# A 64-byte pad ahead of the weight pool in a one-core hybrid decoder block

## Chip, cores and metric

The kernel runs on one core of a Trainium2 chip. The metric is device time in microseconds (us) of one execution. Before the change it is 2321.66 us, the median of three runs (2320.70 to 2322.68).

## What is computed

A decoder block over 256 tokens of width 2048: a SwiGLU feed-forward half step, a gated merge of differential attention and a gated linear recurrence, a second feed-forward half step, and a gated embedding. Cut to its matrix products:

```python
x = x + 0.5 * swiglu(rmsnorm(x, g1), w_gate, w_up, w_down)     # 2048 -> 2 x 5632 -> 2048
proj = rmsnorm(x, g2) @ w_in                                   # 2048 -> 11264
y_a = diff_attention(q, k, v) @ w_branch_a                     # 1024 -> 2048
y_b = hgrn2(hq, hf, hi, hg) @ w_branch_b                       # 1024 -> 2048
x = x + (sigmoid(gate_a) * y_a + sigmoid(gate_b) * y_b) @ w_out
x = x + 0.5 * swiglu(rmsnorm(x, g3), w_gate2, w_up2, w_down2)
x = x + sigmoid(rmsnorm(x, g4) @ w_ple_gate) * rmsnorm(p @ w_ple_proj, g5)
```

Everything is float32. The weights are about 420 MB, and each is read once.

## The kernel before

**The weight stream.** All weights are read in one order of use, the list `plan`, in groups of 256 input rows by 512 output columns (512 KB). `prep` (L103) handles one group: SyncE starts a DMA into `raw`, ScalarE rounds it into `wh` (L114), and VectorE writes the rounding remainder into `wl` (L115). It runs three groups ahead of their use (`AHEAD`). The pool `wp`, which holds five buffers of `raw` and four each of `wh` and `wl`, is the second pool that the program opens; the first, `base`, holds what lives through the whole program.

**The product.** An activation is split in the same way into a rounded part and a remainder, both transposed so that features stand on partitions: `AH`/`AL` for the normed stream, `hH`/`hL` for the hidden layer of a feed-forward, `yaH`/`yaL` and `ybH`/`ybL` for the branch inputs, `mH`/`mL` for the merged branches, `pH`/`pL` for the embedding input. `group` (L141 to L150) then issues, for each k-tile of 128 features and each of the two tiles of 128 tokens, three matmuls into the same 128x512 accumulator: `wh` under the activation's rounded part (L148), `wl` under the same (L149), `wh` under its remainder (L150). So a group is 12 matmuls. The activation slice of 128x128 is the stationary operand, which a weight load (LDWEIGHTS) puts into the array ahead of each matmul; the weights, 512 columns of float32r or 2048 bytes on each partition, are the moving operand. `product` strings the groups of one 512-column chunk together; `last_product` does the very last chunk partly in 256-column halves.

**Side work.** Everything else (scaling of accumulators, transposes, attention, recurrence) is cut into generator tasks. One piece of each runs between two groups of the stream (`advance`), so TensorE has the next group's matmuls queued behind it. The order is written out by the program, engine by engine; no scheduler changes it.

**Where tiles lie.** A pool gives each tag a place in SBUF in the order in which the tags first appear, in steps of 32 bytes per partition, and the pools follow each other. A tile keeps one byte offset on all 128 partitions. The lines that the change touches are L295 and L296, where the first `AH`/`AL` pair and `ss4` are made in `base`, and L335, where `gsub` is made in the pool `mid`.

Of the kernel before, what the change touches and what calls it, by code (L numbers as in the profile page):

```python
# [20 lines left out]
P = 128  # L21
# [27 lines left out]
def block_kernel(ctx: ExitStack, tc: tile.TileContext, a: dict, out: bass.AP):  # L49
# [3 lines left out]
    base = ctx.enter_context(tc.tile_pool(name="base", bufs=1))  # L53
# [8 lines left out]
    def T(pool, shape, tag, dt=F32, **kw):  # L62
        uid[0] += 1
        return pool.tile(shape, dt, tag=tag, name=f"{tag}_{uid[0]}", **kw)
# [4 lines left out]
    def ccol(c):  # L69
        return slice(c * NB, (c + 1) * NB)  # L70

# [1 line left out]
    plan = []  # L73

    def add(w, chunks, groups):
# [39 lines left out]
            nc.vector.tensor_tensor(wl[:, ks, :], raw[:, ks, :], wh[:, ks, :].bitcast(F32), op=ALU.subtract)  # L115
        ready[n] = (wh, wl)

# [1 line left out]
    tasks = []  # L119
    owed = [False]  # L120

# [55 lines left out]
                group(at[0] + i, act, 2 * groups - 1, [d])  # L177
            yield d

# [1 line left out]
    def split(H, L, src, gain=None):  # L181
        if gain is None:
            nc.scalar.copy(H, src)  # L183
            nc.vector.tensor_tensor(L, src, H.bitcast(F32), op=ALU.subtract)  # L184
        else:
            nc.scalar.activation(H, src, AF.Copy, scale=gain)  # L186
            nc.vector.scalar_tensor_tensor(L, src, gain, H.bitcast(F32), op0=ALU.mult, op1=ALU.subtract)
# [34 lines left out]
    def new_act():  # L222
        return T(base, [P, KD, SEQ], "AH", F32R), T(base, [P, KD, SEQ], "AL", F32R)

    def new_ss4():
        return T(base, [P, NT, 4], "ss4", bufs=2)
# [20 lines left out]
    def ffn(gu, down, act, gain_next):  # L247
        with tc.tile_pool(name=gu, bufs=1) as fp:
            hH = T(fp, [P, DFF // P, SEQ], "hH", F32R)
            hL = T(fp, [P, DFF // P, SEQ], "hL", F32R)  # L250

            def hidden(acc, c):
                if c == 0 and rs[0] is None:
                    early = T(fp, [P, NT, NB], "early")
                    for tt in range(NT):
                        nc.scalar.copy(early[:, tt, :], acc[tt])
                    acc = [early[:, tt, :] for tt in range(NT)]
                while rs[0] is None:
                    yield
                h = []  # L260
                for tt in range(NT):
                    s = T(fp, [P, HALF], "s", bufs=2)
                    nc.scalar.activation(s, acc[tt][:, :HALF], AF.Silu, scale=rs[0][:, tt : tt + 1])  # L263
                    h.append(T(fp, [P, HALF], "h", bufs=4))
                    nc.vector.scalar_tensor_tensor(  # L265
                        h[tt], acc[tt][:, HALF:], rs[0][:, tt : tt + 1], s, op0=ALU.mult, op1=ALU.mult
                    )
                yield
                two_k_tiles(lambda tt, kt: h[tt][:, (kt - 2 * c) * P : (kt - 2 * c + 1) * P], hH, hL, 2 * c)

            for c in range(DFF // HALF):
                acc = product(gu, c, KG, act)
                spawn(hidden(acc, c))
            nact = new_act()
            ss4 = new_ss4()
            for c in range(D // NB):
                acc = product(down, c, FG, (hH, hL))
                spawn(residual(acc, c, 0.5, ss4, nact, gain_next, set_rs if c == 3 else None))
        return nact

    # ------------------------------------------------------------------ first FFN
    gains = T(base, [P, 4, KD], "gains")
    nc.sync.dma_start(gains, a["gains"])
    neghalf = T(base, [P, 16], "neghalf")
# [8 lines left out]
    ident = T(base, [P, P], "ident")  # L293
    x = T(base, [P, NT, D], "x")
    act = new_act()  # L295
    ss4 = new_ss4()  # L296

    def load_xT(g):
# [26 lines left out]
    spawn(first_sums())  # L325
    act = ffn("gu1", "down1", act, gains[:, G_MIX])

    # ------------------------------------------------------------------ token mixing
    mid = ctx.enter_context(ExitStack())
    mp = mid.enter_context(tc.tile_pool(name="mid", bufs=1))  # L330
    GA = T(mp, [P, NT, D], "GA")
    V = T(mp, [P, NT, NH * VD], "V")
    yaH = T(mp, [P, NH, SEQ], "yaH", F32R)
    yaL = T(mp, [P, NH, SEQ], "yaL", F32R)
    gsub = T(mp, [P, 1], "gsub")  # L335
    nc.vector.tensor_scalar(gsub, small[:, S_SUB : S_SUB + 1], 1.0 - LAMBDA_INIT, None, op0=ALU.mult)

    def mix(m):
# [27 lines left out]
    with tc.tile_pool(name="att", bufs=1) as ap:  # L366
        qT = T(ap, [P, NH, SEQ], "qT")
        kT = T(ap, [P, NH, SEQ], "kT")
        dv = T(ap, [P, NT, NH * VD], "dv")
        bias = T(ap, [P, NH, SEQ], "bias")  # L370
# [55 lines left out]
                yield  # L426
            have.add(key)

        # the queries of a tile stand in reversed order from qT to aT, as the rows of the bias do
        PARTS = ((0, slice(0, SEQ), slice(0, SEQ)), (1, slice(SEQ, 3 * P), slice(P, SEQ)))  # L430

        def head(h, ya):
# [304 lines left out]
            spawn(residual(acc, c, 1.0, ss4, act, gains[:, G_FFN2], set_rs if c == 3 else None))  # L737
    mid.close()

    # ------------------------------------------------------------------ second FFN  # L740
    act = ffn("gu2", "down2", act, gains[:, G_PLE])

    # ------------------------------------------------------------------ per-layer embedding
    with tc.tile_pool(name="ple", bufs=1) as pp:
        pT = T(pp, [P, 2, SEQ], "pT")
        nc.gpsimd.dma_start(pT, a["pT"])
# [49 lines left out]
        drain()  # L796


# [1 line left out]
def _blocks(w):  # L800
    k, n = w.shape
    return np.ascontiguousarray(w.reshape(k // (2 * P), 2, P, n // NB, NB).transpose(3, 0, 2, 1, 4))


def _gate_up(gate, up):
    k, n = gate.shape
    both = np.stack([gate.reshape(k, n // HALF, HALF), up.reshape(k, n // HALF, HALF)], axis=2)
    return _blocks(both.reshape(k, 2 * n))


def _feature_major(w):
    n, m = w.shape
    return np.ascontiguousarray(w.reshape(n // P, P, m).transpose(1, 0, 2))
# [12 lines left out]
def _constants():  # L826
    j = np.arange(TOEP)
    dist = SEQ - 1 - j
    hot = np.zeros((BUCKETS + 1, TOEP), np.float32)
    ok = dist >= 0  # L830
    hot[_buckets(dist)[ok], j[ok]] = 1.0
    hot[BUCKETS, ~ok] = NEG
    s = np.arange(P)[:, None]
    t = np.arange(64)[None, :]
    masks = np.stack([(s // (2 * m) == t // m) & (s % (2 * m) < m) for m in LEVELS], axis=1).astype(np.int32)
    return hot, masks


def _layout(v):
    v = {k: np.asarray(w) for k, w in v.items()}  # L840
    hot, masks = _constants()
    f = lambda w: np.ascontiguousarray(w)  # noqa: E731
    x = v["x"][0]
    gains = np.stack([v[n][0].reshape(KD, P).T for n in ("ffn1_norm", "mix_norm", "ffn2_norm", "ple_gate_norm")], axis=1)
    small = np.stack(
        [np.tile(v["q_norm"][0], 2), np.tile(v["k_norm"][0], 2), v["diff_subln"][0], v["hgrn_norm"][0]], axis=1
    )
    return {
        "xT": _feature_major(f(x.T)),
        "x": f(x),  # L850
        "pT": _feature_major(f(v["p"][0, 0].T)),
        "gains": f(gains),
        "small": f(small),
        "ident": np.eye(P, dtype=np.float32),
        "flip": f(np.eye(P, dtype=np.float32)[::-1]),
        "rel_bias": f(v["rel_bias"]),
        "onehot": hot,
        "masks": masks,
        "lambdas": f(np.stack([v[n][0] for n in ("lambda_q1", "lambda_q2", "lambda_k1", "lambda_k2")])),
        "lb": f(v["hgrn_lb_logits"].reshape(2, NH, P).transpose(2, 0, 1)),  # L860
        "ple_post": f(v["ple_post_norm"][0]),
        "gu1": _gate_up(v["ffn1_w_gate"][0], v["ffn1_w_up"][0]),
        "down1": _blocks(v["ffn1_w_down"][0]),
        "w_in": _blocks(v["w_in"][0]),
        "w_a": _blocks(v["w_branch_a"][0]),
        "w_b": _blocks(v["w_branch_b"][0]),
        "w_out": _blocks(v["w_out"][0]),
        "gu2": _gate_up(v["ffn2_w_gate"][0], v["ffn2_w_up"][0]),
        "down2": _blocks(v["ffn2_w_down"][0]),
        "w_pg": _blocks(v["w_ple_gate"][0]),  # L870
        "w_pp": _blocks(v["w_ple_proj"][0]),
    }


def build(arrays):
    import concourse.bacc as bacc

    nc = bacc.Bacc("TRN2", target_bir_lowering=False, num_devices=1)
    aps = {
        n: nc.dram_tensor(f"in_{n}", w.shape, mybir.dt.from_np(w.dtype), kind="ExternalInput").ap()  # L880
        for n, w in arrays.items()
    }
    out = nc.dram_tensor("out_y", (SEQ, D), F32, kind="ExternalOutput").ap()
    with tile.TileContext(nc) as tc:
        block_kernel(tc, aps, out)
    return nc
# [9 lines left out]
```

## Time and profile before

| What | Value |
|---|---|
| Median of three runs | 2321.66 us |
| Profiled execution, from first to last instruction | 2320.3 us |
| Mean granted TensorE clock over it | 1.000 |
| Matmul records / weight load records | 10564 / 10564 |
| First matmul of the weight stream starts | 5.5 us |
| First feed-forward, `AH` part, then `hH` part | 5.5 to 502.9, to 745.8 us |
| Mixing, with `AH`, `yaH`, `ybH`, then `mH` | 745.8 to 1478.8 us |
| Second feed-forward, `AH` part, then `hH` part | 1478.8 to 1972.7, to 2215.5 us |
| Embedding, with `AH` and `pH` | 2215.5 to 2315.7 us |
| Last output landed | 2320.3 us |

The profile states no time of its own for the profiled execution beyond its span. The median of the runs is 1.4 us longer than the span; that is what lies around it. In the rows of the trace, a matmul is shown as `accumulator<-moving,stationary`, a start in us, and a duration. Matmuls overlap in the pipeline, so the pace of a stretch is the distance from the start of one to the start of the next, not the duration.

### The profile page before, as it was taken

How to read it: one execution, taken by the hardware profiler on the slowest of the kernel's cores; microseconds unless marked ns; L12 is line 12 of the kernel's file. 1: busy time of each engine (PE TensorE's matmuls, PEld its weight loads, DVE VectorE, ACT ScalarE, POOL GpSimd, SP SyncE). 2: the span in 40 equal slices, each digit the busy share in tenths (PEclk: the TensorE clock that was granted, in tenths of full speed). 3: DMA queues.
4: the chain of work that ended last, by engine and by line, in shares of the span. 5: the costliest groups of instructions: out<-in, count | busy, mean ns of one | idle time of the engine just before them, and what ended most of it. 6: DMA issues, size and time to landing. Idle time of an engine off the chain costs nothing.

```text
span 2320.3 us, 27206 instructions
## 1 busy us (share of the span) xinstructions
PE 2312.7 (100%) x10564; PEld 1903.2 (82%) x10564; DVE 1270.9 (55%) x1381; ACT 1042.7 (45%) x1270; POOL 39.5 (2%) x38
## 2 busy tenths in 40 slices
PE   9999999999999999999999999999999999999999
PEld 7888888888888888888888888888888888888887
DVE  5554555554444576667765555555555554444456
ACT  6444444444444455543344444544444444444454
POOL 0000000000000100000010000000000000000000
PEclk9999999999999999999999999999999999999999
DMA  8655555566666645554455655565555556666664
GB/s 292 190 182 191 190 188 185 189 189 188 188 188 196 201 161 167 186 173 153 160 156 181 186 186 181 179 193 184 189 190 185 188 188 190 193 188 191 188 213 149
DMA packets 120464, 432.55 MB, mean 186 GB/s; under 512 B 13773, under 2 KB 14181, under 8 KB 120208
## 3 DMA queue, kind: packets, MB, share of 16 engines
q1 hardware_dynamic: 118800, 426.33, 58.3%
q0 software_dynamic: 1248, 4.43, 0.5%
q8 instruction: 82, 1.34, 0.2%
q14 instruction: 46, 0.38, 0.0%
q10 hardware_dynamic: 288, 0.07, 0.0%
HBM read 428.67 MB, written 2.11 MB: 186 GB/s over the span
## 4 chain that ended last, share of the span: by engine, by line
PE 99%; DMA 1%; DVE 0%; ACT 0%; SPq 0%; issue 0%; ACTq 0%; DVEq 0%
PE acc L148 32%; PE acc L150 31%; PE acc L149 31%; PE tp L209 1%; PE ms L616 1%; DMA raw<-in_gu 0%; PE tp L219 0%; PE ms L440 0%; PE ms L150 0%; PE ms L149 0%; PE ms L148 0%; PE ms L589 0%; PE tp L362 0%; DMA junk<-in_xT 0%; PE tp L477 0%; PE ms L641 0%
## 5 line engine op out<-in xcount | busy, mean ns | idle before, releaser
L115 DVE TENSOR_TENSOR wl<-raw,wh 128x1024 fp32r<-128x1024 f32 (+1 forms) x805 | 983.9, 1223 | 888.9 <-ACT wh L114 886.5
L114 ACT CAST wh<-raw 128x1024 fp32r<-128x1024 f32 (+1 forms) x805 | 844.9, 1051 | 941.1 <-PE acc L150 915.6
L148 PE MATMUL acc<-wh,AH 128*128 128x512 f32 x2224 | 885.2, 398 | 0.2 <-ACT wh L114 0.2
L150 PE MATMUL acc<-wh,AL 128*128 128x512 f32 x2224 | 872.3, 392 | 0.0
L149 PE MATMUL acc<-wl,AH 128*128 128x512 f32 x2224 | 866.9, 390 | 1.6 <-DVE wl L115 1.6
L150 PEld LDWEIGHTS acc<-wh,AL 128*128 128x128 f32 x2224 | 417.7, 188 | 95.5
L149 PEld LDWEIGHTS acc<-wl,AH 128*128 128x128 f32 x2224 | 418.1, 188 | 91.5 <-DVE wl L115 3.7
L148 PEld LDWEIGHTS acc<-wh,AH 128*128 128x128 f32 x2224 | 418.4, 188 | 84.7 <-ACT wh L114 1.7
L148 PE MATMUL acc<-wh,hH 128*128 128x512 f32 x704 | 275.3, 391 | 0.0
L150 PE MATMUL acc<-wh,hL 128*128 128x512 f32 x704 | 274.2, 390 | 0.0
L149 PE MATMUL acc<-wl,hH 128*128 128x512 f32 x704 | 273.9, 389 | 0.0
L150 PEld LDWEIGHTS acc<-wh,hL 128*128 128x128 f32 x704 | 132.1, 188 | 27.8
L149 PEld LDWEIGHTS acc<-wl,hH 128*128 128x128 f32 x704 | 132.2, 188 | 27.1
L148 PEld LDWEIGHTS acc<-wh,hH 128*128 128x128 f32 x704 | 132.2, 188 | 27.1
L263 ACT ACTIVATE s<-acc,rowr 128x256 f32<-128x256 f32 x86 | 40.8, 477 | 49.9 <-PE acc L150 49.9
L183 ACT CAST hH<-tp 128x512 fp32r<-128x512 f32 x44 | 25.8, 587 | 74.7 <-PE tp L209 74.7
L184 DVE TENSOR_TENSOR hL<-tp,hH 128x512 fp32r<-128x512 f32 x44 | 30.4, 692 | 46.6 <-ACT hH L183 46.5
L265 DVE SCALAR_TENSOR_TENSOR h<-acc,rowr,s 128x256 f32<-128x256 f32 x86 | 41.4, 483 | 20.6 <-ACT s L263 20.6
L148 PE MATMUL acc<-wh,mH 128*128 128x512 f32 x128 | 51.3, 401 | 0.0
L149 PE MATMUL acc<-wl,mH 128*128 128x512 f32 x128 | 50.6, 395 | 0.0
L150 PE MATMUL acc<-wh,mL 128*128 128x512 f32 x128 | 50.6, 395 | 0.0
L186 ACT ACTIVATE AH<-tp,gains 128x256 fp32r<-128x256 f32 x48 | 22.9, 477 | 31.0 <-PE tp L209 16.9
(191 smaller groups left out, 1019.9 us busy)
## 6 DMA issues: line engine op xcount, KB each, us to landing
raw<-in_gu SPq DMA_DIRECT2D x351, 512.0 KB, 3.5
raw<-in_down SPq DMA_DIRECT2D x176, 512.0 KB, 3.8
raw<-in_w_in SPq DMA_DIRECT2D x176, 512.0 KB, 3.6
raw<-in_w_out SPq DMA_DIRECT2D x32, 512.0 KB, 3.7
raw<-in_w_pg SPq DMA_DIRECT2D x32, 512.0 KB, 4.3
raw<-in_w_a SPq DMA_DIRECT2D x16, 512.0 KB, 3.5
raw<-in_w_b SPq DMA_DIRECT2D x16, 512.0 KB, 3.5
junk<-in_xT SPq DMA_DIRECT2D x8, 256.0 KB, 4.2
```

The costliest lines, as they stand in the source:

```text
L114: nc.scalar.copy(wh[:, ks, :], raw[:, ks, :])
L115: nc.vector.tensor_tensor(wl[:, ks, :], raw[:, ks, :], wh[:, ks, :].bitcast(F32), op=ALU.subtract)
L148: nc.tensor.matmul(dst, hi, wh[:, k2, cols], start=(kt == 0), stop=False)
L149: nc.tensor.matmul(dst, hi, wl[:, k2, cols], start=False, stop=False)
L150: nc.tensor.matmul(dst, lo, wh[:, k2, cols], start=False, stop=(kt == last))
L183: nc.scalar.copy(H, src)
L184: nc.vector.tensor_tensor(L, src, H.bitcast(F32), op=ALU.subtract)
L186: nc.scalar.activation(H, src, AF.Copy, scale=gain)
L209: nc.tensor.transpose(tp[:, i, tcol(tt)], src_of(tt, kt + i), ident)
L263: nc.scalar.activation(s, acc[tt][:, :HALF], AF.Silu, scale=rs[0][:, tt : tt + 1])
L265: nc.vector.scalar_tensor_tensor(h[tt], acc[tt][:, HALF:], rs[0][:, tt : tt + 1], s, op0=ALU.mult, op1=ALU.mult)
L616: nc.tensor.matmul(lp[:, i, tt, :], km[:, i, tt, :], q4[:, i, tt, :], start=True, stop=True)
```

## The change

An unused tile of 64 bytes per partition is made in `base` behind the first `AH`/`AL` pair, and `gsub` is made 8 elements wide, of which the first is used. The rest of the diff takes comments out.

```diff
@@ -293,6 +293,7 @@
     ident = T(base, [P, P], "ident")
     x = T(base, [P, NT, D], "x")
     act = new_act()
+    T(base, [P, 16], "trail")
     ss4 = new_ss4()
...
-    gsub = T(mp, [P, 1], "gsub")
+    gsub = T(mp, [P, 8], "gsub")[:, 0:1]
```

Each engine has the same instructions in the same order as before, on the same buffers; names carry a number that is one higher, and lines below L295 move down by one. `gsub` has a slot of 32 bytes either way, so nothing moves for it. What moves are the addresses in SBUF: every tile that comes behind the first `AL` lies 64 bytes later on its partition. In the two built programs:

| Tile | Role in the matmuls | Byte offset before | Modulo 128 before | Modulo 128 now |
|---|---|---|---|---|
| `ident` | moving, in transposes | 17920 | 0 | 0 |
| `x` | stationary, in transposes | 18432 | 0 | 0 |
| `AH`, `AL` | stationary | 34816, 51200 | 0 | 0 |
| `raw`, five buffers | none | 72768 and on | 64 | 0 |
| `wh`, four buffers | moving | 93248 and on | 64 | 0 |
| `wl`, four buffers | moving | 109632 and on | 64 | 0 |
| `hH`, `hL` | stationary | 126016, 171072 | 64 | 0 |
| `pH`, `pL` | stationary | 136256, 138304 | 64 | 0 |
| `yaH`, `yaL` | stationary | 150592, 158784 | 64 | 0 |
| `ybH`, `ybL` | stationary | 175200, 183392 | 96 | 32 |
| `mH`, `mL` | stationary | 191584, 207968 | 96 | 32 |

Buffers of one tag lie 4096 bytes apart, the two k-tiles of a weight group 2048, and the slices of an activation 512, so every operand of a row keeps that row's residue.

## Prediction

> **What bounds the kernel now.** I read the page's head first, then the chain that ended last, then TensorE's waits, then the groups of the weight stream.
>
> ```profile
> span 2320.3 us, 27206 instructions
> PE 2312.7 (100%) x10564; PEld 1903.2 (82%) x10564; DVE 1270.9 (55%) x1381; ACT 1042.7 (45%) x1270; POOL 39.5 (2%) x38
> PE 99%; DMA 1%; DVE 0%; ACT 0%; SPq 0%; issue 0%; ACTq 0%; DVEq 0%
> PE acc L149 <- DVE wl L115: 1.6, 3, 0.8
> PE ms L290 <- DVE warm L287: 1.2, 1, 1.2
> PE acc L148 <- ACT wh L114: 0.2, 1, 0.2
> ```
>
> The chain that ended last is TensorE for 99% of the span. The last three rows are all that TensorE waited for: 1.6 + 1.2 + 0.2 = 3.0 us in 2320.3. So the time is the number of matmuls times their pace, and nothing can be gained by earlier data. The change alters no instruction and no order, only addresses; it can act only through that pace, or by slowing another engine until TensorE waits for it.
>
> The second comes first. These rows are the two engines and the DMA that feed one group of 12 matmuls:
>
> ```profile
> L115 DVE TENSOR_TENSOR wl<-raw,wh 128x1024 fp32r<-128x1024 f32 (+1 forms) x805 | 983.9, 1223 | 888.9 <-ACT wh L114 886.5
> L114 ACT CAST wh<-raw 128x1024 fp32r<-128x1024 f32 (+1 forms) x805 | 844.9, 1051 | 941.1 <-PE acc L150 915.6
> raw<-in_gu SPq DMA_DIRECT2D x351, 512.0 KB, 3.5
> ```
>
> Twelve matmuls at the paces found below take 12 x 226.7 ns = 2.72 us or more. VectorE needs 1.22 us of that and ScalarE 1.05, and a DMA lands 3.5 us after its issue while three groups are prepared ahead. This cover is why I cost any change in these engines at nothing: if the addresses made VectorE's subtraction slower, it would have to go from 1.22 to above 2.6 us before a matmul waited.
>
> **The pace, by the residue of the operands.** The pace must be read from starts, in stretches where nothing stands between the matmuls of one product. For each kind of stationary operand I took the first and last row of such a stretch in the timeline of TensorE.
>
> ```profile
> 753.34 0.39 PE L149 MATMUL acc<-wl,AH 128*128 128x512 f32 x1
> ...
> 779.89 0.39 PE L148 MATMUL acc<-wh,AH 128*128 128x512 f32 x1
> 1976.32 0.40 PE L150 MATMUL acc<-wh,hL 128*128 128x512 f32 x1
> ...
> 2016.68 0.39 PE L148 MATMUL acc<-wh,hH 128*128 128x512 f32 x1
> 1221.71 0.39 PE L150 MATMUL acc<-wh,yaL 128*128 128x512 f32 x1
> ...
> 1247.58 0.39 PE L150 MATMUL acc<-wh,yaL 128*128 128x512 f32 x1
> 1272.51 0.40 PE L149 MATMUL acc<-wl,ybH 128*128 128x512 f32 x1
> ...
> 1283.01 0.40 PE L149 MATMUL acc<-wl,ybH 128*128 128x512 f32 x1
> 1415.95 0.40 PE L150 MATMUL acc<-wh,mL 128*128 128x512 f32 x1
> ...
> 1434.15 0.40 PE L150 MATMUL acc<-wh,mL 128*128 128x512 f32 x1
> ```
>
> They stand for 117, 179, 115, 46 and 79 matmuls, so 116, 178, 114, 45 and 78 steps. `AH`: 26.55 us / 116 = 228.9 ns. `hH`: 40.36 / 178 = 226.7. `yaH`: 25.87 / 114 = 226.9. `ybH`: 10.50 / 45 = 233.3. `mH`: 18.20 / 78 = 233.3. The moving operand is at 64 modulo 128 throughout. The stationary one is at 0 in the first stretch, at 64 in the next two, at 96 in the last two. Two tiles at the same residue but tens of KB apart have one pace (`hH` and `yaH`; `ybH` and `mH`), while the three residues have three. So the pace follows the address modulo 128, not the place in SBUF, the stage, or what the other engines do meanwhile. In words: operands at the **same residue** cost 226.8 ns (the mean of the two), 64 bytes apart 228.9, 32 bytes apart 233.3.
>
> That the stationary operand matters at all is plain from how its load lies:
>
> ```profile
> 753.57 0.39 PE L150 MATMUL acc<-wh,AL 128*128 128x512 f32 x1
> 753.57 0.19 PEld L148 LDWEIGHTS acc<-wh,AH 128*128 128x128 f32 x1
> 753.80 0.39 PE L148 MATMUL acc<-wh,AH 128*128 128x512 f32 x1
> ```
>
> The load for the matmul at 753.80 starts with the matmul before it, at 753.57, and takes 0.19 us: both operands are read from SBUF at the same time, and the 0.23 us to the next start outlast the load.
>
> **The change part by part.** Three kinds of streams have to be costed, by these counts (the two other lines of `group` have the same):
>
> ```profile
> L148 PE MATMUL acc<-wh,AH 128*128 128x512 f32 x2224 | 885.2, 398 | 0.2 <-ACT wh L114 0.2
> L148 PE MATMUL acc<-wh,hH 128*128 128x512 f32 x704 | 275.3, 391 | 0.0
> L148 PE MATMUL acc<-wh,mH 128*128 128x512 f32 x128 | 51.3, 401 | 0.0
> L148 PE MATMUL acc<-wh,ybH 128*128 128x512 f32 x64 | 25.3, 396 | 0.0
> L148 PE MATMUL acc<-wh,yaH 128*128 128x512 f32 x64 | 25.3, 395 | 0.0
> L148 PE MATMUL acc<-wh,pH 128*128 128x512 f32 x16 | 6.2, 389 | 0.0
> ```
>
> (1) `AH`/`AL`, 3 x 2224 = 6672 matmuls. The moving operand goes from 64 to 0 and the stationary one stays at 0: they were 64 apart and are now at one residue. If the distance sets the pace, it goes from 228.9 to 226.8: 6672 x 2.1 ns = **14.0 us less**. (2) `hH`, `yaH`, `pH`, 3 x (704 + 64 + 16) = 2352 matmuls: both operands move by 64, the distance stays 0, no change. (3) `mH`, `ybH`, 3 x (128 + 64) = 576 matmuls: 64 under 96 becomes 0 under 32, the distance stays 32, no change.
>
> No row of this case has a moving operand of the stream at 0, so the pace of a pair (0, 0) or (0, 32) is bounded, not read. From above by the slowest pair seen, 233.3. From below by the halves in the last chunk:
>
> ```profile
> 2311.43 0.28 PE L149 MATMUL ms<-wl,AH 128*128 128x256 f32 x1
> ...
> 2315.31 0.28 PE L149 MATMUL ms<-wl,AH 128*128 128x256 f32 x1
> ```
>
> These are 34 matmuls of 256 columns, 33 steps in 3.88 us: 117.6 ns. The second 256 columns of a 512-column matmul at 226.7 thus cost 109.1, and twice that is 218.2 ns: what 512 columns would take if all that is paid once per matmul went away. I take 226.8 for (0, 0), because it is the only measured pace of two operands at one residue, and keep 218.2 and 233.3 for the range.
>
> (4) The other matmuls, the float32 ones and the transposes, move too:
>
> ```profile
> L209 PE MATMUL tp<-ident,h 128*128 128x128 f32 x176 | 26.3, 271 | 0.0
> L209 PE MATMUL tp<-ident,x 128*128 128x128 f32 x96 | 14.4, 272 | 0.0
> L589 PE MATMUL ms<-q,k 128*128 128x128 f32 x32 | 4.2, 274 | 0.0
> L641 PE MATMUL ms<-V,A 128*128 128x128 f32 x16 | 3.1, 275 | 0.0
> ```
>
> `h` is at 64, `x` at 0: 271 and 272 ns. `q`, `k` are both at 0, `V` at 64 over `A` at 0: 274 and 275. Durations of one kind differ by 1 ns whatever the residues, and 868 such records are left, so at most 0.9 us either way; I take 0. (5) `gsub` and the comments: nothing moves for them.
>
> The sum against the profiled execution is 2320.3 - 14.0 = 2306.3. With the 1.4 us by which the median exceeds the span it is **2307.7 us**, 0.6% less. TensorE stays the bound.
>
> **Rivals.** *A: the moving operand alone costs a part of every matmul.* A read of 2048 bytes that starts at 64 modulo 128 touches 17 pieces of 128 bytes, and 226.7 / 17 x 16 = 213.4: the excess would be one piece more than needed. For it: the exact 17 to 16, and that about 9 ns per matmul is paid once. Against it: by the same count the half would touch 9 pieces, 120.0 ns, and it takes 117.6. If it holds, every stream falls to about the lower bound: 6672 x (228.9 - 218.2) + 2352 x (226.8 - 218.2) + 576 x (233.3 - 6.5 - 218.2) = 71.4 + 20.2 + 5.0 = 96.6 us less, 2225 us (the 6.5 is what a distance of 32 costs over none). With half of that gone it is 2273. Twelve matmuls would take 2.62 us, still over VectorE's 1.22. The Trainium skill, "TensorE: Matmul & The Clock Gate", section "Back-to-back issue gap", gives 512 / 2.4 + 2.5 = 215.8 ns for such a matmul; as an estimate, by this every stream at 215.8 would take 2204 us, and no run here shows that pace.
>
> *B: the stationary residue counts by itself, not the distance.* Then `AH` stays at 228.9; `hH`, `yaH` and `pH` come to 0 and take 228.9 as well, 2352 x 2.1 = 4.9 us more; `mH` and `ybH` at 32 take between 226.8 and 233.3, 0 to 3.7 us less. That is 2322.9 to 2326.6. The rows above can't tell this from the distance, since the moving operand never varies.
>
> *C: slower, since two reads that start at the head of one 128-byte piece collide.* The matmul and the next weight load start together; where both start at 0 each step, they may meet as the pair 32 apart does now. What speaks against it is that the pair (64, 64) starts just as close and is the fastest. Today's mean over the 9024 matmuls of (1) and (2) is (6672 x 228.9 + 2352 x 226.8) / 9024 = 228.4 ns: above that pace for (0, 0) the change is slower, and above 228.9 by more than 0.2%. At 233.3 it is 6672 x 4.4 + 2352 x 6.5 = 44.6 us more, 2366.
>
> *D: nothing changes.* A shift by 64 bytes keeps each operand's place in any unit of 64 or fewer bytes; were the differences above due to something that goes with the tiles but isn't their address, the time would be 2321.7. The two pairs of distant tiles with one pace speak against it. The Trainium skill, "SBUF — State Buffer", section "Specifications (TRN2)", counts SBUF lines as 16 bytes, by which 64 bytes more change nothing; the three paces at residues 0, 64 and 96 disagree, since all three are multiples of 16. That the change doesn't do what it says is ruled out by the addresses of the two programs.
>
> **How the numbers follow.** Distance sets the pace, 2307.7 us: 0.32. A: 0.30, from 2179 (all at the 213.4 of 16 pieces, 142.6 us less) over 2225 to 2273. B: 0.20, of which two thirds end within 0.2% and one third above. C: 0.12. D: 0.06. A measurement of this kernel tells about 0.2%, 4.6 us, from no change. Faster: 0.32 + 0.30 = 0.62. Within: 0.13 + 0.06 = 0.19. Slower: 0.07 + 0.12 = 0.19. The range takes in the forecast, B, D and most of A, from 2200 to 2332, and leaves out C's larger sizes and the far end of A. The forecast's own range is 2303 to 2312.
>
> **What would show it.** The steps to read are the same five stretches. Forecast: `AH` at 226.8, `hH` and `yaH` still at 226.8, `ybH` and `mH` still at 233.3. A: `hH` below 224, and the half below 117. B: `AH` still at 228.9, `hH` up to 228.9. C: `AH` and `hH` both above 228.9. Wrong altogether would be a difference that comes from waits of TensorE, above the 3.0 us of now, or from VectorE's 1223 ns.

## The result and the profile after

The changed kernel takes 2347.36 us (median of 4 runs, 2346.63 to 2347.96) against 2321.53 us before (4 runs, the three of above and one more). The ratio is 1.0109, with a 95% interval of 1.0097 to 1.0122: it is 1.1% **slower**. The profiled span goes from 2320.3 to 2345.0 us, by 24.7.

The waits of TensorE in the changed kernel come first (engine, line and what it waited for, then us in total, times, longest):

```profile
PE acc L149 <- DVE wl L115: 1.8, 4, 0.8
PE ms L290 <- DVE warm L287: 1.2, 1, 1.2
PE acc L148 <- ACT wh L114: 0.4, 1, 0.4
```

That is 3.4 us where it was 3.0, so the time did not come from a wait. The same stretches as in the prediction, from the timeline of TensorE in the changed kernel, first and last row each (start in us, duration, line, `accumulator<-moving,stationary`):

```profile
761.11 0.39 PE L149 MATMUL acc<-wl,AH 128*128 128x512 f32 x1
...
788.06 0.40 PE L148 MATMUL acc<-wh,AH 128*128 128x512 f32 x1
1999.40 0.40 PE L149 MATMUL acc<-wl,hH 128*128 128x512 f32 x1
...
2039.80 0.39 PE L150 MATMUL acc<-wh,hL 128*128 128x512 f32 x1
1286.03 0.40 PE L149 MATMUL acc<-wl,ybH 128*128 128x512 f32 x1
...
1296.53 0.40 PE L149 MATMUL acc<-wl,ybH 128*128 128x512 f32 x1
1407.17 0.39 PE L150 MATMUL acc<-wh,mL 128*128 128x512 f32 x1
...
1425.36 0.40 PE L150 MATMUL acc<-wh,mL 128*128 128x512 f32 x1
```

They are 117, 179, 46 and 79 matmuls. `AH`: 26.95 us / 116 steps = 232.3 ns, where it was 228.9. `hH`: 40.40 / 178 = 227.0, as before. `ybH`: 10.50 / 45 = 233.3, as before. `mH`: 18.19 / 78 = 233.2, as before. Of these only the stream over `AH`/`AL` became slower, and `AH` and `AL` are the only stationary operands of the stream whose place relative to the moving one changed. By stage, from the starts of the first matmuls of each part:

| Part | Before, us | After, us | Difference |
|---|---|---|---|
| First feed-forward, `AH` | 497.4 | 504.7 | +7.3 |
| First feed-forward, `hH` | 242.9 | 242.9 | 0.0 |
| Mixing (`AH`, `yaH`, `ybH`, `mH`) | 733.0 | 739.8 | +6.8 |
| Second feed-forward, `AH` | 493.9 | 502.7 | +8.8 |
| Second feed-forward, `hH` | 242.8 | 242.9 | 0.0 |
| Embedding (`AH`, `pH`) | 100.2 | 101.6 | +1.4 |

The differences sum to 24.3 of the 24.7 us, or 3.6 ns for each of the 6672 matmuls over `AH`/`AL`; the other 0.4 us is a later start of the stream. Added up over the whole trace, the steps from one matmul over `AH`/`AL` to the next grew by 24.2 us, and all other steps of TensorE together by 0.5. The order of the program and the clock (1.000) are as before.

The stretch shown is one of the faster ones. Here is another, from the first feed-forward of the changed kernel, of 94 matmuls:

```profile
103.31 0.40 PE L150 MATMUL acc<-wh,AL 128*128 128x512 f32 x1
...
125.01 0.39 PE L150 MATMUL acc<-wh,AL 128*128 128x512 f32 x1
```

21.70 us / 93 = 233.3 ns. A stretch below is any unbroken sequence of 30 or more matmuls over one kind of activation from 60 us on, without its first two. By these, the pace over `AH` was 228.9 to 229.2 ns before and is 232.2 to 233.5 now; in 56 of the 72 stretches over `AH` of the changed kernel it is 233 or more.

### The profile page after: what moved, and what is told of

Read it like the earlier page. It is cut to its first block, busy times and chain, and to the rows that moved or that the text cites. A ratio compares the mean times of both kernels' runs of the same rounds, so it can differ in the third digit from the quotient of the medians.

```text
span 2345.0 us, 27206 instructions
## 1 busy us (share of the span) xinstructions
PE 2337.0 (100%) x10564; PEld 1903.7 (81%) x10564; DVE 1271.4 (54%) x1381; ACT 1040.1 (44%) x1270; POOL 39.4 (2%) x38
## 4 chain that ended last, share of the span: by engine, by line
PE 98%; DMA 1%; DVE 0%; ACT 0%; SPq 0%; issue 0%; ACTq 0%; DVEq 0%
PE acc L148 31%; PE acc L150 31%; PE acc L149 31%; PE tp L209 1%; PE ms L617 1%; DMA raw<-in_gu 1%; PE tp L219 0%; PE ms L441 0%; PE ms L150 0%; PE ms L148 0%; PE ms L149 0%; PE ms L590 0%; PE tp L363 0%; ACT wh L114 0%; PE ms L642 0%
## 5 line engine op out<-in xcount | busy, mean ns | idle before, releaser
L115 DVE TENSOR_TENSOR wl<-raw,wh 128x1024 fp32r<-128x1024 f32 (+1 forms) x805 | 983.9, 1223 | 906.9 <-ACT wh L114 904.7
L149 PE MATMUL acc<-wl,AH 128*128 128x512 f32 x2224 | 878.4, 395 | 1.8 <-DVE wl L115 1.8
```

The lines of the kernel that those rows point to most:

```text
L149: nc.tensor.matmul(dst, hi, wl[:, k2, cols], start=False, stop=False)
```

## Experiments

Distance below means the byte offset of the moving operand minus that of the stationary one, by the addresses of each built program. Theory 1, formed after the result: this distance sets the pace, with a period larger than 128 bytes. Before the change the weights lie 64 bytes from `AH` modulo 256, now 128; modulo 128 that looked like 0. In the cuts of the edits below, a line `trail` that is taken out is the changed kernel's. The other cuts are against the kernel that the text names, or else the one before.

**Undoing the change of distance alone: the pad ahead of `AH`.**

```diff
+    T(base, [P, 16], "lead")
     act = new_act()
-    T(base, [P, 16], "trail")
```

> The 64-byte pad stands ahead of AH and AL instead of behind them, so the weights, hH, yaH and the rest lie where the changed kernel has them, and AH and AL move along. Theory 1, the distance from stationary to moving operand modulo more than 128 sets the pace: AH is again 64 short of the weights, pace 228.9 ns, hH 226.8, time 2321.5 us (2318 to 2325), the same as before. Rival, the own address of the moving operand (0 modulo 128 now) slows the AH streams: AH stays at 233.1 ns, time 2347 us.

2321.79 us, ratio to before 1.000 (0.9991 to 1.001). Two rows of its timeline, 116 matmuls from first to last:

```profile
753.09 0.40 PE L150 MATMUL acc<-wh,AL 128*128 128x512 f32 x1
...
779.42 0.39 PE L148 MATMUL acc<-wh,AH 128*128 128x512 f32 x1
```

26.33 us / 115 = 229.0 ns. The weights lie exactly where the changed kernel has them, at 0 modulo 128, and `AH` is at 64; the pace is the one before the change. So the own address of the moving operand isn't what slowed `AH`.

**Other pads behind `AL`.**

```diff
-    T(base, [P, 16], "trail")
+    T(base, [P, 112], "trail")
```

> The pad behind AL has 448 bytes instead of 64, so that the weights lie a multiple of 512 bytes from AH (and at 0 modulo 128, as in the changed kernel). Theory 1 with modulus 512 or 256: AH now has hH's distance, pace 226.8 ns, 6672 x 2.1 = 14 us less than before, 2307.5 us (2304 to 2311). Rival, moving and stationary operand both at 0 modulo 128 is what slows AH: as in the changed kernel, 233.1 ns and 2347 us.

2311.20 us, ratio 0.9954 (0.9939 to 0.9969). 116 matmuls:

```profile
748.64 0.40 PE L150 MATMUL acc<-wh,AL 128*128 128x512 f32 x1
...
774.75 0.39 PE L148 MATMUL acc<-wh,AH 128*128 128x512 f32 x1
```

26.11 / 115 = 227.0 ns. Weights and `AH` both start at 0 modulo 128, as in the changed kernel, and the streams are now faster than before the change; so the collision of two operands at 0 isn't the cause. The time is 0.2 us above the top of what was expected: the stretches over `AH` pace 226.7 to 227.8 ns, not 226.8 throughout.

The pad of 48 elements, 192 bytes:

> A pad of 192 bytes: the weights lie 256 modulo 512 from AH. Theory 1 with modulus 256: same as a distance of 0, 226.8 ns and 2307.5 us. Theory 1 with modulus 512: a pace of its own, not seen so far; any value from 226 to 240 ns, most likely as slow as 233 or slower, 2348 us or more. Rival, both at 0 modulo 128 is slow: 233.1 ns, 2347 us.

2310.60 us, ratio 0.9951 (0.9934 to 0.9967), the same as with 448 bytes, and the stretches over `AH` again pace 226.7 to 227.8 ns. Distances of 256 and of 0 modulo 512 cost the same. And on the slow side, a pad of 80 elements, 320 bytes:

> A pad of 320 bytes, 256 more than the change has: distance of AH 384, which is 128 modulo 256. Theory 1 with modulus 256: the same as the changed kernel, AH near 233.1 ns, 2347 us (2344 to 2350). Rival, the modulus is 512 and 0 and 256 merely cost the same: another pace and time.

2347.11 us, ratio 1.0108 (1.0092 to 1.0125), the changed kernel's time again, and its paces over `AH`, 232.2 to 233.5 ns. Two pads 256 bytes apart gave one time, twice: the distances repeat after **256 bytes**. That they repeat after 128 already is ruled out by the change itself, since 0 and 128 differ.

**Is it `AH`, or the distance? No pad in `base`, but `hH` and `hL` moved in their own pool.**

```diff
+            T(fp, [P, 96 if gu == "gu1" else 112], "shift")
             hH = T(fp, [P, DFF // P, SEQ], "hH", F32R)
```

> No pad behind AL; instead hH and hL are moved within their pool, by 384 bytes in the first feed-forward (moving minus stationary is 128 modulo 512, as AH in the changed kernel) and by 448 in the second (64, as AH before). Theory 1, the distance counts whatever the tile: hH paces 232.4 to 233.6 ns in the first and 228.9 in the second, 1056 x 6.2 + 1056 x 2.1 = 8.8 us more, 2330 us (2327 to 2334); AH stays at 228.9. Rival, AH is special (its place in SBUF or its stage): both hH paces stay at 226.8 and the time at 2321.5 us.

2330.58 us, ratio 1.0039 (1.0024 to 1.0054), as theory 1 gave it. The first pair of rows is from the first feed-forward (172 matmuls), the second from the second (175):

```profile
506.25 0.39 PE L149 MATMUL acc<-wl,hH 128*128 128x512 f32 x1
...
545.98 0.40 PE L149 MATMUL acc<-wl,hH 128*128 128x512 f32 x1
1981.96 0.40 PE L149 MATMUL acc<-wl,hH 128*128 128x512 f32 x1
...
2021.80 0.39 PE L149 MATMUL acc<-wl,hH 128*128 128x512 f32 x1
```

39.73 / 171 = 232.3 ns and 39.84 / 174 = 229.0 ns. One other stretch of the first feed-forward paces 233.3, as most do over `AH` in the changed kernel; those over `AH` itself stay at 228.9 to 229.2. Moving `hH` and `hL` (and the small tiles behind them in their pool) gives them `AH`'s paces at the same two distances. This shows the cause as far as addresses go: another tile, another stage, weights unmoved.

**A map of more distances.** `AH` at 32, `hH` at 96 and 160, `ybH` and `mH` at 192, by pads of 224 bytes behind `AL`, of 160 and 96 ahead of `hH` in the two feed-forwards, and of 32 ahead of `ybH`.

> Four distances (moving minus stationary, modulo 256) that no run has shown: AH at 32, hH at 96 in the first feed-forward and at 160 in the second, ybH and mH at 192. If a distance and its negative cost the same (only how far apart the two reads are counts): 32 as 224, so AH 233.3 ns; 192 as 64, so ybH and mH 228.9; 96 and 160 alike. If the order of the two reads counts: 32 differs from 233.3 or 192 from 228.9. If what matters is being a multiple of 64: 32, 96 and 160 slow (about 233), 192 fast (227 to 229). Time mainly by AH: 6672 x (233.3 - 228.9) = 29 us more than before if 233.3.

2363.22 us, ratio 1.0178 (1.0159 to 1.0197). In order, `AH` (116 matmuls), `hH` of the first (169) and second feed-forward (176), `mH` (80):

```profile
769.23 0.40 PE L150 MATMUL acc<-wh,AL 128*128 128x512 f32 x1
...
796.06 0.40 PE L148 MATMUL acc<-wh,AH 128*128 128x512 f32 x1
515.61 0.39 PE L150 MATMUL acc<-wh,hL 128*128 128x512 f32 x1
...
554.81 0.39 PE L150 MATMUL acc<-wh,hL 128*128 128x512 f32 x1
2008.81 0.39 PE L150 MATMUL acc<-wh,hL 128*128 128x512 f32 x1
...
2049.80 0.40 PE L148 MATMUL acc<-wh,hH 128*128 128x512 f32 x1
1439.48 0.39 PE L150 MATMUL acc<-wh,mL 128*128 128x512 f32 x1
...
1457.91 0.40 PE L148 MATMUL acc<-wh,mH 128*128 128x512 f32 x1
```

233.3, 233.3, 234.2 and 233.3 ns. 32 costs what 224 costs, but 192 doesn't cost what 64 costs, so a distance and its negative can differ; nor are multiples of 64 fast as such, since 192 isn't. Over all stretches of this and the other runs so far, with the version at the end:

| Distance modulo 256 | 0 | 32 | 64 | 96 | 128 | 160 | 192 | 224 |
|---|---|---|---|---|---|---|---|---|
| Pace, ns | 226.7 to 227.8 | 233.2 to 233.4 | 228.9 to 229.2 | 233.3 | 232.2 to 233.5 | 234.2 | 233.3 to 233.4 | 233.2 to 233.4 |

0 is the lowest of these, and 64, where `AH` stood before the change, the next: the change moved the largest group of matmuls away from the second best place.

This order is that of matmuls of 512 columns. The halves of 256 columns in the last chunk, over `AH` as well, have another. In the version at the end, at distance 0:

```profile
2295.43 0.28 PE L148 MATMUL ms<-wh,AH 128*128 128x256 f32 x1
...
2299.62 0.28 PE L150 MATMUL ms<-wh,AL 128*128 128x256 f32 x1
```

These are 36 matmuls, 4.19 us / 35 = 119.7 ns, where the kernel before had 117.6 at distance 64. In the changed kernel, at 128, the halves take 118.7, and in the run of this map, at 32, 116.7: for them 0 is the slowest of these four distances and 32 the fastest.

**Does each matmul pay for itself? `AH` at 0, `AL` at 128.** A pad of 64 bytes behind `AL` and a gap of 128 between the two:

```diff
     def new_act():
-        return T(base, [P, KD, SEQ], "AH", F32R), T(base, [P, KD, SEQ], "AL", F32R)
+        H = T(base, [P, KD, SEQ], "AH", F32R)
+        T(base, [P, 32], "gap")
+        return H, T(base, [P, KD, SEQ], "AL", F32R)
```

> A gap of 128 bytes between AH and AL: AH is at distance 0, AL at 128. While the matmul of line 149 (under AH) runs, AL is loaded for the next; while those of lines 150 (under AL) and 148 (under AH) run, AH is loaded. If the pace is set by the load of the next stationary operand that reads beside the running matmul: the steps from line 149 to 150 are long (232 to 235 ns), the two others near 227. If it is set by the matmul's own stationary operand: the steps from 150 to 148 are long. Mean of the three near 228.5 to 229.5 either way, time 2318 to 2325 us.

2336.09 us, ratio 1.0061 (1.0043 to 1.008). Neither case came out. Consecutive rows:

```profile
404.31 0.40 PE L150 MATMUL acc<-wh,AL 128*128 128x512 f32 x1
404.55 0.39 PE L148 MATMUL acc<-wh,AH 128*128 128x512 f32 x1
404.77 0.40 PE L149 MATMUL acc<-wl,AH 128*128 128x512 f32 x1
405.00 0.40 PE L150 MATMUL acc<-wh,AL 128*128 128x512 f32 x1
405.24 0.39 PE L148 MATMUL acc<-wh,AH 128*128 128x512 f32 x1
```

From line 148 to 149 it is 0.22 us, from 149 to 150 0.23, from 150 to 148 0.24, twice: both the step in which `AL` is loaded and the one in which it stands in the array are long. Over `AH` and `AL` the stretches pace 230.9 to 231.7 ns, more than the 229 that one slow step in three would give, and the time is 11 us above the range.

The same from the other side: `AH`, `AL` and `wh` as with the pad of 192, but `wl` moved by 128 bytes.

```diff
+        if n == 0:
+            T(wp, [P, 32], "gap", bufs=1)
         wl = T(wp, [P, 2, NB], "wl", F32R)
```

> Pad of 192 bytes, and a gap of 128 bytes between the buffers of wh and wl, so that under AH the matmuls of lines 148 and 150 run at distance 0 and that of line 149 at 128; under hH the other way round, 148 and 150 at 128 and 149 at 0. If each matmul pays for its own distance alone: under AH only the steps from line 149 to 150 are long (232 to 234 ns), the other two near 227, mean 229; under hH only those from 149 are short, mean 231. If a long step also lengthens the next, as the steps from line 150 in the run with AL apart suggest: under AH the steps from 149 and from 150 are both long, mean 231, and under hH at most one in three is short. Time by the first 6672 x 1.7 + 2112 x 4 + 576 x 0 = 20 us over the pad of 192 alone, 2330 us; by the second 6672 x 4 + 2112 x 4 = 35 us over it, 2346 us.

2347.99 us, ratio 1.0111 (1.009 to 1.0131). A stretch over `AH` (116 matmuls; the copy of the program is two lines longer, so lines 148 to 150 are 150 to 152) and one over `hH` (178):

```profile
761.46 0.39 PE L152 MATMUL acc<-wh,AL 128*128 128x512 f32 x1
...
788.29 0.40 PE L150 MATMUL acc<-wh,AH 128*128 128x512 f32 x1
512.46 0.39 PE L152 MATMUL acc<-wh,hL 128*128 128x512 f32 x1
...
552.97 0.39 PE L152 MATMUL acc<-wh,hL 128*128 128x512 f32 x1
```

233.3 ns over `AH`, where two of three matmuls are at distance 0, and 228.9 over `hH`, where two of three are at 128. In 30 of the 72 stretches over `AH` it is about 231.1 instead, as in these 94 matmuls:

```profile
126.23 0.39 PE L152 MATMUL acc<-wh,AL 128*128 128x512 f32 x1
...
147.72 0.39 PE L152 MATMUL acc<-wh,AL 128*128 128x512 f32 x1
```

21.49 us / 93 = 231.1 ns. The time came near the second expectation's 2346 us, but not by its steps: `hH` didn't slow to the pace that it gives. A mean of the single prices (229 and 231) is too low for `AH` and too high for `hH`, so a step doesn't go by its own distance alone. What rule joins them stays open.

**Distances between the steps of 32 bytes.** As the pad of 192, with `hH` and `hL` 16 bytes off.

> As the pad of 192, with hH and hL 16 bytes off the 32-byte steps: distance 16 in the first feed-forward, 240 in the second. If the two reads collide in pieces of 32 bytes or more: a pace like that at 32 or 224 bytes for one or both (about 233). If in smaller ones or by the multiple of 16 alone: 226.8 for both. Time 2310.6 to 2324 us accordingly (2112 x 6.5 = 13.7).

2315.39 us, ratio 0.9972 (0.9959 to 0.9984). The offset of `hH` is 16 modulo 256 in the first feed-forward and 240 in the second, and the weights are at 0. So by moving minus stationary the distance is 240 in the first and 16 in the second, the other way round than the expectation has it. Two stretches of the first feed-forward, at one and the same distance of 240 (174 and 170 matmuls):

```profile
501.71 0.39 PE L149 MATMUL acc<-wl,hH 128*128 128x512 f32 x1
...
540.93 0.39 PE L148 MATMUL acc<-wh,hH 128*128 128x512 f32 x1
565.47 0.40 PE L150 MATMUL acc<-wh,hL 128*128 128x512 f32 x1
...
604.91 0.39 PE L148 MATMUL acc<-wh,hH 128*128 128x512 f32 x1
```

39.22 / 173 = 226.7 ns in the first 512-column chunk, 39.44 / 169 = 233.4 in the second. The four chunks of this stage take 226.7, 233.3, 233.3 and 226.7 ns, so one distance has two paces, and each holds for a chunk of some 60 us. In the second feed-forward, at 16, all four chunks take 228.3. Neither expectation is met, though the time lies in the range given.

**The version that follows.** Pad of 192 bytes, and 224 bytes ahead of `ybH`, which puts all stationary operands of the stream at distance 0.

```diff
-    T(base, [P, 16], "trail")
+    T(base, [P, 48], "trail")
...
+        T(gp, [P, 56], "shift")
         ybH = T(gp, [P, NH, SEQ], "ybH", F32R)
```

> Pad of 192 bytes behind AL, and 224 bytes ahead of ybH in its pool, so that ybH, ybL, mH and mL come to distance 0 modulo 256 as well. Theory 1 with modulus 256: ybH and mH pace 226.8 instead of 233.3, 576 x 6.5 = 3.7 us less than with the pad of 192 alone, 2307 us (2304 to 2309), the fastest so far. If instead those two tiles were slow for another reason: 2310.6 us.

2306.84 us (2306.37 to 2308.64, 5 runs), ratio to before 0.9937 (0.9924 to 0.9951). `AH` (117 matmuls) and `ybH` (46):

```profile
748.20 0.40 PE L149 MATMUL acc<-wl,AH 128*128 128x512 f32 x1
...
774.52 0.39 PE L148 MATMUL acc<-wh,AH 128*128 128x512 f32 x1
1264.96 0.39 PE L148 MATMUL acc<-wh,ybH 128*128 128x512 f32 x1
...
1275.16 0.39 PE L148 MATMUL acc<-wh,ybH 128*128 128x512 f32 x1
```

26.32 us / 116 = 226.9 and 10.20 / 45 = 226.7 ns. The 3.7 us expected of `ybH` and `mH` came: 2310.60 to 2306.84. This beats both kernels, by a pad as idle as the change's own.

## Why the prediction was wrong

**That the pace alone decides** was right: waits 3.4 us, VectorE's subtraction at 1223 ns as before, `hH`, `ybH` and `mH` at their old paces. That it goes by the distance of the two operands, not by their own addresses, was right as well: the pad ahead of `AH` and the moved `hH` show it.

**The step that failed** is the price in part (1), "they were 64 apart and are now at one residue". The residue was taken modulo 128, from three paces at residues 0, 64 and 96. That modulus was read from the rows only as far as they go: among the streams before the change no two had distances 128 apart modulo 256, so nothing there could tell 128 from 256. Modulo 256 the change moves `AH` from 64 to 128, and its pace went from 228.9 to between 232.2 and 233.5 ns, not to 226.8. The term of 14.0 us less became 24.3 us more, and the sum 2307.7 became 2347. The size was nearly right for the distance it named: the pads of 192 and 448 bytes, which do bring `AH` to 0, gave 2310.6 and 2311.2, 11 us less than before in place of 14, at paces of 226.7 to 227.8 in place of 226.8.

**Parts (2) and (3)**, no change for streams whose operands move together, held to 0.3 ns in the three tiles shown. **Part (4)** held: outside the weight stream, the steps of TensorE sum to the same in both traces within 0.1 us.

**Rivals.** A, the moving operand's start at 64: dead, since `hH` has it at 0 now and still paces 227.0 ns. The lower bound of 218.2 takes the halves over `AH`, 64 apart, from the pace of `hH`, 0 apart; from `AH`'s own 228.9 it is 222.6. No stretch of 512 columns came below 226.7. The estimate of 2204 us beside it is a slip of the sum: 9600 matmuls at 215.8 ns in place of the measured paces come to 2198. And the section that it names, "Back-to-back issue gap" on the page "TensorE: Matmul & The Clock Gate" of the Trainium skill, gives 215.8 for a matmul by itself, not for a stream with a weight load ahead of each as here. B, the stationary residue by itself: dead, since `hH` came to 0 without becoming slower. C, the collision of two starts at 0 modulo 128: right on the sign and near on the pace of `AH`, but by luck. It has `hH` slow as well, which stayed at 227.0 with both starts at 0, and with the pads of 192 and 448 bytes `AH` still starts with the weights at 0 and is fast. D, no change: dead by the 1.1%.

**The range** ended at 2332 because a slow pair (0, 0) was held to need a collision, and `hH` at (64, 64) spoke against that. The slowest pace seen, 233.3 ns, was the right upper bound for `AH`, to 0.2 ns; the 0.12 put on the slow side was too little for a pair that no row showed.

## What to carry to other kernels

Where matmuls follow each other without waits, look at the pace by kind of stationary operand and set it against the offset of the two operands in SBUF. Aligning each one by itself isn't the point: for these float32r matmuls of 512 columns, each with its own weight load, the distance between the two modulo 256 bytes decided. A pad of 64 bytes cost 1.1%, and 192 bytes won 0.5%. The halves of 256 columns had another order, so other shapes need a measurement of their own. A period read from a few residues is a guess until two addresses that it calls equal have been compared.

## What the runs showed of the hardware

The Trainium skill, "TensorE: Matmul & The Clock Gate", section "Step-by-step: what each phase is for", says that TensorE reads the moving and the stationary operand through two independent ports, so that loading the next weights takes no read bandwidth from the running matmul. The trace disagrees as far as the pace goes: with the weights where they were, moving `hH` and `hL` took the steps from 226.8 to 232.3 ns. Where in the chip the two meet was not tried.

One distance can have two paces: with `hH` 16 bytes off, one chunk ran at 226.7 ns and the next at 233.4, in one kernel, and at a distance of 128 stretches ran at 232.2 to 232.6 or at 233.3 to 233.5. What sets the one or the other stays open. Mixed distances don't average either (231.1 or 233.3 ns where two in three matmuls are at the best distance). So the pace is read from whole stretches, several of them, and a price per matmul is used only where all matmuls are alike.
